# Turning the query tiles by VectorE's 32x32 squares and by their writes, in a hybrid attention layer

## The chip, the cores and the metric

One core of a Trainium2 chip runs the whole layer. The metric is the device time of one execution in microseconds (us).

## The reference

One layer of a diffusion backbone, in float32. A prompt tile of 128 tokens and 1024 latent tokens (eight tiles of 128) go through a modulated RMS norm and one input projection, whose columns belong to two mixers with 8 query heads, 2 key heads and head size 64 each. Mixer A attends over all latent and cached keys, mixer B within a window of 128 and the cached keys. The query part is this:

```python
p = h @ w_in
q_a, k_a, v_a, g_a, q_b, k_b, v_b, g_b = jnp.split(p, SPLIT_IDX, axis=-1)
q_a = rmsnorm(q_a.reshape(b, t, N_HEADS_A, HEAD_DIM), qn_a)      # the same for q_b
q_a = apply_rope(q_a, cos, sin)                                  # latent tokens alone
s = jnp.einsum('bqkgd,bskd->bkgqs', qblk, k_all) * (d ** -0.5)   # 4 query heads for each key head
p = jax.nn.softmax(s, axis=-1)
o = jnp.einsum('bkgqs,bskd->bqkgd', p, v_all)
```

The gated outputs of both mixers go through one output projection and are added to the stream.

## The kernel before

**Precision.** Float32 operands are split into a high part, rounded for TensorE's fast float32 format (`F32R`), and a low part, the rest. A product is made of three matmuls: high by high, high by low, low by high.

**Stages.** Modulation and the turned inputs (`hT`); the gates of mixer A; the query stage, 18 blocks (9 tiles for mixer A, then 9 for B, each time the tiles 1 to 8 and the prompt, tile 0, last); 9 key and value blocks; the gates of mixer B; then the attention in 36 units (tile, mixer, key head), with the output projection woven in.

**Order.** Nothing is reordered: at the end `in_order` ties every engine's instructions, the DMA issues of SyncE's queue among them, to the order in which the program wrote them. That order comes from an agenda. `block` counts two ticks, at the head and in the middle of its 24 matmuls (8 slices of the inner dimension by three), and `later(n, f)` runs `f` at the n-th tick from now. So a step of tile k is written between the matmuls of a later block. What a block of another weight needs (`split`: a high part by ScalarE, a low part by VectorE, 8 of each) is written into the last block of the weight before.

**A query tile** (`query`). The projection of 128 tokens by 8 heads by 64 lies in PSUM (`pq`). Its steps follow at the ticks of `QUERY_AT`, counted from one tick after the block:

- `squares` (0): ScalarE squares, VectorE sums them per head (`ss`, L717) and scales (`ms`, L184), GpSimd takes the power -1/2 (`rs_q`, L186).
- `scale` (2): VectorE multiplies by it (`qn`, L722) and makes the products with the rotation's tables (`ra` L657, `rb` L663).
- `rotated` (3): VectorE adds them into `qf` (L733), heads in pairs.
- `turned` (6): TensorE turns `qf` in four transposes of 128x128 into the bank `ptq` (L743), ScalarE copies the high part out (`qo0`, L746), two DMAs from ScalarE's queue write it to `q_dram`; one tick later VectorE subtracts the low part (`qo1`, L751), and after two more ScalarE's queue writes it in two DMAs.

The last tile of mixer B uses `QUERY_LAST` in place of `QUERY_AT`. So at any time three or four tiles are under way, and in a block VectorE works on one tile's `qn`, `ra`, `rb`, the next one's sum and an older one's `qf` and low part. `pq` rotates over six banks, `qf` over three buffers, `qo0` and `qo1` over two each.

`q_dram[t][m]` has 128 rows: 64 high and 64 low ones, one per element of a head; its columns are two groups of 512, one for each key head. A group is four heads of 128 tokens, head by head.

**Loads within the stage.** All are issued by SyncE's queue. At the head of the last but one block of mixer A (block 7) the program writes: two loads of the gate weights `wg` (1 MB each, L703), their bias (L777), the eight slices `rawqb` of mixer B's query weights (256 KB each, L234) and mixer B's rotation tables `tcos` and `tsin` (L671); two ticks later VectorE multiplies the tables by the gains (L672). The same place in mixer B has the 16 loads of `rawkv`. In blocks 12 and 16 stand the gate rows (`pgate` on TensorE, L696, and a sum of four steps on VectorE, L689).

**A unit** loads its group of `q_dram` (`u_load`, L977) into `qtile`, 128 rows by 512. For mixer A the running maxima (`pmx`, L997) take a head's 128 columns as the stationary operand; the scores (`st`, L1333 and L1334) stream all 512 columns against the keys, and their exponentials, times the values, give `pv`, 512 columns in the same order. `gated` (L1382) reads `pv` and the inverse sums `rs` by head pair into the output layout. For mixer B the scores (`sn`, L1085 and L1086) take a head's columns as the stationary operand.

Of the kernel before, what the change touches and what calls it, by code (L numbers as in the profile page):

```python
# [9 lines left out]
F32 = mybir.dt.float32  # L10
# [8 lines left out]
P = 128  # L19
D = 1024  # L20
KT = D // P
HD = 64
# [34 lines left out]
TURN = (2, 1)  # L57
PUT_LOW = 2
QUERY_AT = (0, 2, 3, 6)
PAD = 2  # L60
SECOND_FROM = 5
WARM = (12, 2, 1, 3)
# [14 lines left out]
PROMPT_KEYS_AT = 12  # L77
KV_ORDER = [0] + list(range(1, NT))
GATE_AT = (3, 7)
QUERY_LAST = (0, 1, 2, 5)  # L80
CACHE_AT = 8
VC_AT = 6
ONES_AT = 14
# [34 lines left out]
def hybrid_step(ctx, tc, x_prompt, x_sample, cache_k_a, cache_v_a, cache_k_b, cache_v_b,  # L118
# [100 lines left out]
    class Weights:  # L219
# [36 lines left out]
        def split(self):  # L256
            self.split_high()
            self.split_low()
# [418 lines left out]
    with tc.tile_pool(name="qt", bufs=2, side="right") as qt:  # L677
# [29 lines left out]
        def query(pq, m, t, tabs, n=1):  # L707

            nm = f"q{m}_{t}"
            pqv = pq.rearrange("p (h d) -> p h d", d=HD)  # L710
            v = {}

            def squares():
                sq = qt.tile([P, 8, HD], F32, tag="sq", name=f"sq{nm}")
                nc.scalar.activation(sq, pqv, AF.Square)
                ss = qt.tile([P, 8], F32, tag="ss", name=f"ss{nm}")
                nc.vector.tensor_reduce(ss, sq, axis=AX.X, op=ALU.add)  # L717
                v["r"] = rsqrt_mean(qt, ss, HD, 8, nm)

            def scale():  # L720
                qn = qt.tile([P, 8, HD], F32, tag="qn", name=f"qn{nm}")
                nc.vector.tensor_tensor(qn, pqv, v["r"].unsqueeze(2).to_broadcast([P, 8, HD]), op=ALU.mult)  # L722
                v["qn"] = qn
                if t:
                    v["rot"] = rope_products(qt, qn, 8, *tabs[m], t, nm)

            def rotated():

                qf = qt.tile([P, 4, 2, HD], F32, tag="qf", name=f"qf{nm}", bufs=3)
                out = qf.rearrange("p h g d -> p g h d")  # L730
                pair = lambda a: a.rearrange("p (g h) d -> p g h d", g=2)
                if t:
                    nc.vector.tensor_tensor(out, *(pair(a) for a in v["rot"]), op=ALU.add)  # L733
                else:
                    nc.vector.tensor_tensor(
                        out, pair(v["qn"]), gain4[:, 2 * m, :].unsqueeze(1).unsqueeze(1).to_broadcast([P, 2, 4, HD]),
                        op=ALU.mult)
                v["qf"] = qf

            def turned():  # L740
                ptq = bank_tr(f"pt{nm}")
                for h in range(4):
                    nc.tensor.transpose(ptq[:, P * h : P * h + P], v["qf"][:, h].rearrange("p g d -> p (g d)"),  # L743
                                        ident_r.bitcast(F32))
                qo = [qt.tile([P, 512], F32R, tag=f"qo{i}", name=f"qo{i}{nm}") for i in range(2)]
                nc.scalar.copy(qo[0], ptq)  # L746
                put(qo[0], 0)
                later(1, lambda: low(ptq, qo))

            def low(ptq, qo):  # L750
                nc.vector.tensor_tensor(qo[1], ptq, qo[0], op=ALU.subtract)  # L751
                later(PUT_LOW, lambda: put(qo[1], 1))

            def put(part, i):
                for g in range(2):
                    nc.scalar.dma_start(q_dram[t][m][64 * i : 64 * i + 64, 512 * g : 512 * g + 512],
                                       part[64 * g : 64 * g + 64].bitcast(F32))

            for d, f in zip(QUERY_LAST if (m, t) == (1, 0) else QUERY_AT, (squares, scale, rotated, turned)):
                later(n + d, f)  # L760

        tabs = {0: rope_tables(qt, 0, 2)}
# [210 lines left out]
    def u_load(i):  # L973
# [3 lines left out]
        nc.sync.dma_start(qt_.bitcast(F32), q_dram[t][m][:, 512 * g : 512 * g + 512])  # L977
        qtile[i] = qt_

    def max_items(i):  # L980

        t, m, g = units[i]
        out = []

        def item(h, b):
            if h == 0 and b == 0:
                mxtile[i] = qs.tile([P, 4, 3], F32, tag="mx", name=f"mx{i}", bufs=3)
            mx = mxtile[i]
            lhs = qtile[i][:, P * h : P * h + P]
            pm = bank("B" if i == APART + 1 else "A", f"pmx{i}_{h}_{b}")  # L990
            if t == 0:
                for h in range(4):
                    hs = slice(P * h, P * h + P)
                    nc.tensor.matmul(pm[:, hs], qtile[i][:, hs], khb[:, g, 0, :], start=True, stop=True)
                nc.vector.tensor_reduce(mx[:, :, 0], pm.rearrange("p (h n) -> p h n", h=4), axis=AX.X, op=ALU.max)
            else:
                nc.tensor.matmul(pm[:, 0:384], lhs, kha[:, g, 3 * b : 3 * b + 3, :], start=True, stop=True)  # L997
                nc.vector.tensor_reduce(mx[:, h, b : b + 1], pm[:, 0:384], axis=AX.X, op=ALU.max)  # L998

        def finish():  # L1000
            qb_ = qp.tile([68, 512], F32R, tag="qb", name=f"qb{i}", bufs=2)
            nc.sync.dma_start(qb_[0:64, :].bitcast(F32), q_dram[t][m][0:64, 512 * g : 512 * g + 512])
            qbtile[i] = qb_
            mx = mxtile.pop(i)
            mn = m_nat[i // 2 % 2]
            nc.vector.tensor_reduce(mn, mx if t else mx[:, :, 0:1], axis=AX.X, op=ALU.max)
            later(TURN[boxed(t)], transpose)

        def transpose():
            pt = bank("E" if i in EARLY else "A", f"ptm{i}")  # L1010
            nc.tensor.transpose(pt[0:4, 0:P].bitcast(F32R), m_nat[i // 2 % 2], ident_r)
            nc.vector.tensor_tensor(qbtile[i][64:68, :].rearrange("p (h n) -> p h n", h=4),
                                    pt[0:4, 0:P].unsqueeze(1).to_broadcast([4, 4, P]),
                                    diag.unsqueeze(2).to_broadcast([4, 4, P]), op=ALU.mult)

        for h in range(4 if t else 1):
            for b in range(3 if t > 0 else 1):
                out.append(lambda h=h, b=b: item(h, b))
        return out, finish

    def boxed(t):

        return t > 1
# [5 lines left out]
    def weight_items(i):  # L1029
# [48 lines left out]
        def item(h, early):  # L1078
            p0, p1_ = window(t)
            n = P * (p1_ - p0)  # L1080
            if i not in penat:
                first(n)
            lhs = qtile[i][:, P * h : P * h + P]
            s = bank("DEEE"[h] if i == 3 else "B" if early else "A", f"sn{i}_{h}")[:, 0:n]
            nc.tensor.matmul(s, lhs, khb[:, g, p0:p1_, :], start=True, stop=False)  # L1085
            nc.tensor.matmul(s, lhs, klb[:, g, p0:p1_, :], start=False, stop=True)  # L1086
            m0 = P if t == 1 else 0

            nc.vector.tensor_tensor_reduce(s, s, mask[:, m0 : m0 + n], -1.0, nsink[:, 4 * g + h : 4 * g + h + 1],  # L1089
                                           op0=ALU.add, op1=ALU.min, accum_out=v["nm"][:, h : h + 1])  # L1090
            later(1, lambda: exp(h, s, -1.0))

        def prompt():
            first(P)
            s = bank("A", f"sn{i}")
            for h in range(4):
                hs = slice(P * h, P * h + P)
                nc.tensor.matmul(s[:, hs], qtile[i][:, hs], khb[:, g, 1, :], start=True, stop=False)
                nc.tensor.matmul(s[:, hs], qtile[i][:, hs], klb[:, g, 1, :], start=False, stop=True)
            mx = small("mx4")  # L1100
            nc.vector.tensor_reduce(mx, s.rearrange("p (h n) -> p h n", h=4), axis=AX.X, op=ALU.max)
            nc.vector.scalar_tensor_tensor(v["nm"], mx, -1.0, nsink[:, 4 * g : 4 * g + 4], op0=ALU.mult, op1=ALU.min)
            for h in range(4):
                exp(h, s[:, P * h : P * h + P], 1.0)
# [242 lines left out]
    def values(i, b, last, blk, ph, pl):  # L1347
# [26 lines left out]
        def gated():  # L1374
            rs = v["rs"]
            o = 768 + 256 * (i % 3)
            of = spare[:, o : o + 256].rearrange("p (c n) -> p c n", c=2)
            a = 4 if m and boxed(t) else 1
            pvv, srv = (x.rearrange("p (c a s n) -> p s c a n", c=2, a=a, s=2) for x in (pv[0:64, :], rs))
            ofv = of.rearrange("p c (a n) -> p c a n", a=a)  # L1380
            for s in range(2):
                nc.vector.tensor_tensor(ofv[64 * s : 64 * s + 64], pvv[:, s], srv[:, s],  # L1382
                                        op=ALU.add if m else ALU.mult)
            nc.gpsimd.tensor_tensor(of, of, sgl.pop(i), op=ALU.mult)
            later(GATE_LATE, lambda: load_gate(i + 2 + (i + 2 >= APART)))
            if i + 3 == APART:
                later(GATE_LATE, lambda: load_gate(APART))
            v["of"] = of
# [208 lines left out]
```

## Time and profile before

| | |
|---|---|
| median of 3 runs | 685.09 us (681.66, 685.09, 685.44) |
| the profiled execution | 684.31 us, its span 682.5 us, granted clock 0.999 |
| busy: TensorE, VectorE, ScalarE, GpSimd | 671.6, 492.9, 403.9, 374.3 us |
| query stage's transposes L743 | 72, first at 103.0, last at 205.8 us |
| VectorE in 100 to 155 and 155 to 208 us | 42.43 of 55, 42.16 of 53 us busy |
| DMA engines in these two stretches | 0.38 and 0.60 busy |

In the profile's rows PE is TensorE's matmuls, PEld its stationary loads, DVE is VectorE, ACT ScalarE, POOL GpSimd, SP SyncE; a `q` behind the name is the engine's own queue, where DMAs are issued. A row of a group has its line, engine, operation, output and inputs, shapes and count, then busy us and mean ns, then the idle time before and what ended it. A row of a timeline or of the chain begins with its start in us from the span's start and its length. A row of the waits has who waited for whom: us in total, times, the longest. A row of the windows has the stretch, its length, busy us and instructions of PE, PEld, DVE, ACT and POOL, the granted clock, the share of the DMA engines and GB/s.

### The profile page before, as it was taken

How to read it: one execution, taken by the hardware profiler on the slowest of the kernel's cores; microseconds unless marked ns; L12 is line 12 of the kernel's file. 1: busy time of each engine (PE TensorE's matmuls, PEld its weight loads, DVE VectorE, ACT ScalarE, POOL GpSimd, SP SyncE). 2: the span in 40 equal slices, each digit the busy share in tenths (PEclk: the TensorE clock that was granted, in tenths of full speed). 3: DMA queues.
4: the chain of work that ended last, by engine and by line, in shares of the span. 5: the costliest groups of instructions: out<-in, count | busy, mean ns of one | idle time of the engine just before them, and what ended most of it. 6: DMA issues, size and time to landing. Idle time of an engine off the chain costs nothing.

```text
span 682.5 us, 10639 instructions
## 1 busy us (share of the span) xinstructions
PE 671.6 (98%) x3325; PEld 535.8 (79%) x3325; DVE 492.9 (72%) x1060; ACT 403.9 (59%) x834; POOL 374.3 (55%) x379
## 2 busy tenths in 40 slices
PE   8999999999999999999999999999999999999987
PEld 4678988878788888997767777877777777777766
DVE  4777247877787882856788788788787877886673
ACT  6656412411233243169778877987798778878760
POOL 2557023332222240248687669767876778778761
PEclk9999999999999999999999999999999999999999
DMA  9961283339445024542266445764565545644623
GB/s 351 405 250 76 79 313 75 78 84 301 120 119 142 29 90 144 183 136 64 81 195 187 154 149 169 195 191 129 162 192 156 154 148 171 201 123 147 185 61 125
DMA packets 75851, 107.74 MB, mean 158 GB/s; under 512 B 9296, under 2 KB 43532, under 8 KB 75796
## 3 DMA queue, kind: packets, MB, share of 16 engines
q1 hardware_dynamic: 67556, 95.11, 43.6%
q10 hardware_dynamic: 8240, 11.96, 6.5%
q8 instruction: 26, 0.43, 0.3%
q14 instruction: 29, 0.24, 0.1%
HBM read 73.24 MB, written 33.80 MB: 157 GB/s over the span
## 4 chain that ended last, share of the span: by engine, by line
PE 92%; DVE 3%; ACT 2%; DMA 1%; issue 1%; POOL 0%; SPq 0%; ACTq 0%; DVEq 0%
PE po L1434 14%; PE pv L1357 7%; PE pv L1354 6%; PE pmx L997 5%; PE pq L270 5%; PE pq L268 5%; PE pq L269 5%; PE pv L1356 5%; PE st L1333 5%; PE st L1334 5%; PE pg L282 3%; PE pg L278 3%; PE pg L283 3%; PE pk L269 2%; PE pk L270 2%; PE pk L268 2%
## 5 line engine op out<-in xcount | busy, mean ns | idle before, releaser
L1344 POOL TENSOR_TENSOR pl<-pe,ph 128x512 fp32r<-128x512 f32 x129 | 167.0, 1301 | 71.8 <-ACT ph L1340 46.0
L998 DVE TENSOR_REDUCE mx<-pmx 128x1 f32<-128x384 f32 x192 | 100.0, 547 | 28.9 <-PE pmx L997 28.8
L1336 ACT ACTIVATE pe<-st 128x512 f32<-128x512 f32 x146 | 86.6, 593 | 12.8 <-PE st L1334 12.0
L1340 ACT CAST ph<-pe 128x512 fp32r<-128x512 f32 x146 | 90.7, 621 | 5.6
L1354 PE MATMUL pv<-ph,v_hi 128*128 128x512 f32 x208 | 82.1, 395 | 0.6 <-DVE spare L1382 0.5
L1357 PE MATMUL pv<-pl,v_hi 128*128 128x512 f32 x208 | 82.2, 395 | 0.2 <-DVE pl L1330 0.2
L186 POOL TENSOR_TENSOR rs_q<-ms_q,mhalf 128x8 f32<-128x8 f32 x18 | 34.2, 1899 | 80.7 <-DVE ms_q L184 80.7
L1434 PE MATMUL po<-wo,ogh 128*128 128x512 f32 (+1 forms) x224 | 73.2, 387 | 0.0
L1055 ACT ACTIVATE pen<-sn,nm 128x512 f32<-128x512 f32 (+2 forms) x72 | 45.0, 626 | 37.3 <-DVE nm L1089 33.5
L1089 DVE CUSTOM_DVE_ANT_0 sn<-sn,mask,nsink 128x512 f32<-128x512 f32 (+1 forms) x64 | 45.9, 717 | 19.3 <-PE sn L1086 12.8
L997 PE MATMUL pmx<-kha,qt 128*128 128x384 f32 x192 | 58.5, 351 | 0.6 <-DVE mx L998 0.6
L1356 PE MATMUL pv<-ph,v_lo 128*64 128x512 f32 x146 | 57.7, 395 | 0.0
L1333 PE MATMUL st<-qt,kha 128*128 128x512 f32 x144 | 57.7, 400 | 0.0
L1334 PE MATMUL st<-qb,kla 68*128 68x512 f32 x144 | 57.4, 398 | 0.0
L1357 PEld LDWEIGHTS pv<-pl,v_hi 128*128 128x128 f32 x208 | 39.1, 188 | 17.5 <-DVE pl L1330 0.6
L997 PEld LDWEIGHTS pmx<-kha,qt 128*128 128x128 f32 x192 | 36.3, 189 | 14.0 <-ACT pen L1055 3.6
L1354 PEld LDWEIGHTS pv<-ph,v_hi 128*128 128x128 f32 x208 | 39.1, 188 | 8.9 <-PE pmx L997 0.9
L1434 PEld LDWEIGHTS po<-wo,ogh 128*128 128x128 f32 x224 | 41.0, 188 | 5.7 <-ACT ogh L1396 0.3
L746 ACT CAST qo0q<-ptq 128x512 fp32r<-128x512 f32 x18 | 10.6, 586 | 57.5 <-PE ptq L743 51.6
L1434 PE MATMUL po<-wo,ogl 128*128 128x512 f32 (+1 forms) x112 | 43.5, 388 | 0.0
L1322 POOL TENSOR_TENSOR pl<-pen,ph 128x512 fp32r<-128x512 f32 x28 | 37.4, 1337 | 7.4 <-ACT ph L1318 7.4
L1065 DVE STREAM_TRANSPOSE pen<-pen 128x512 f32<-128x512 f32 (+1 forms) x56 | 37.0, 677 | 5.8 <-ACT pen L1055 5.7
(258 smaller groups left out, 1721.9 us busy)
## 6 DMA issues: line engine op xcount, KB each, us to landing
td<-pen SPq DMA_DIRECT2D x24, 512.0 KB
pen<-td SPq DMA_DIRECT2D x96, 128.0 KB
qt<-qd SPq DMA_DIRECT2D x36, 256.0 KB
wm<-in_w_mod_ss_dram SPq DMA_DIRECT2D x7, 1024.0 KB
qd<-qo0q ACTq DMA_DIRECT2D x36, 128.0 KB
qd<-qo1q ACTq DMA_DIRECT2D x36, 128.0 KB
sgl<-gd SPq DMA_DIRECT2D x35, 128.0 KB
out_dram<-yt SPq DMA_DIRECT2D x17, 256.0 KB
```

Of the source, the lines that this page charges most:

```text
L268: nc.tensor.matmul(out, h_at(0, i, k, tok), w.hi[k], start=(k == 0), stop=False)
L997: nc.tensor.matmul(pm[:, 0:384], lhs, kha[:, g, 3 * b : 3 * b + 3, :], start=True, stop=True)
L998: nc.vector.tensor_reduce(mx[:, h, b : b + 1], pm[:, 0:384], axis=AX.X, op=ALU.max)
L1333: nc.tensor.matmul(s, kh, qtile[i], start=True, stop=False)
L1334: nc.tensor.matmul(s, kl, qbtile[i], start=False, stop=True)
L1336: nc.scalar.activation(pe, s, AF.Exp)
L1340: nc.scalar.copy(ph, pe)
L1344: nc.gpsimd.tensor_tensor(pl, pe, ph, op=ALU.subtract)
L1354: nc.tensor.matmul(pv, two, ph, start=(b == 0), stop=False)
L1356: nc.tensor.matmul(pv[0:64, :], vl, ph, start=False, stop=False)
L1357: nc.tensor.matmul(pv, two, pl, start=False, stop=last)
L1434: nc.tensor.matmul(po[n, q.start], a, wo_parts[KT * n + k][lo][:, q], start=(k == KS[0] and p == 0), stop=(k == KS[-1] and p == 2))
```

## The change

For the 18 query tiles the transposes on TensorE go. `rotated` now writes `qf` in two adds, one for each key head, with the four heads of a group innermost (a step of four elements between neighbours of one head). `boxes_turned` turns 32x32 squares of it in place on VectorE, taking every fourth element. `split` makes the high part on ScalarE and the low part on GpSimd, both from SBUF. `put_boxes` puts the squares where they belong: four DMAs for each part, one for each 32 tokens, in pieces of 512 bytes, the high part's from ScalarE's queue and the low part's from SyncE's. The steps stand at ticks 0, 2, 3, 4 and 5 (`BOXED_AT`), for the last tile at 0 to 4, and the low put two ticks after the split.

In `q_dram` a group's 512 columns are now tokens with the four heads innermost. `head(i, h)` therefore reads every fourth column of `qtile` as a stationary operand; the maxima's rows in `qbtile` and, for mixer A, the reads of `pv` and `rs` in `gated` follow that order.

```diff
-QUERY_LAST = (0, 1, 2, 5)
+BOXED_AT = (0, 2, 3, 4, 5)
+MIXED = (0, 1)
+QUERY_LAST = (0, 1, 2, 3, 4)
...
             def rotated():
-                qf = qt.tile([P, 4, 2, HD], F32, tag="qf", name=f"qf{nm}", bufs=3)
-                out = qf.rearrange("p h g d -> p g h d")
-                pair = lambda a: a.rearrange("p (g h) d -> p g h d", g=2)
+                qf = qt.tile([P, 512], F32, tag="qf", name=f"qf{nm}", bufs=3)
+                v["qf"] = qf
+                pair = lambda a: a.rearrange("p (g h) (b j) -> p g h b j", g=2, b=2)
+                if m in MIXED:
+                    out = qf.rearrange("p (g b j h) -> p g h b j", g=2, b=2, h=4)
...
+                for g in range(2):
+                    if t:
+                        nc.vector.tensor_tensor(out[:, g], *(pair(a)[:, g] for a in v["rot"]), op=ALU.add)
...
+            def boxes_turned():
+                at = v["qf"].rearrange("p (b x h) -> p b h x", b=4, h=4)
+                nc.vector.transpose(at, at)
+
+            def split():
+                qo = [qt.tile([P, 512], F32R, tag=f"qo{i}", name=f"qo{i}{nm}") for i in range(2)]
+                nc.scalar.copy(qo[0], v["qf"])
+                put_boxes(qo[0], 0, nc.scalar)
+                nc.gpsimd.tensor_tensor(qo[1], v["qf"], qo[0], op=ALU.subtract)
+                later(PUT_LOW, lambda: put_boxes(qo[1], 1, nc.sync))
+
+            def put_boxes(part, i, queue):
+                out = q_dram[t][m][64 * i : 64 * i + 64].rearrange("(b j) (g a x) -> a j g b x", b=2, g=2, a=4)
+                for a in range(4):
+                    src = part[32 * a : 32 * a + 32].bitcast(F32).rearrange("p (g b x) -> p g b x", g=2, b=2)
+                    queue.dma_start(out[a], src)
...
+            if m in MIXED:
+                at, last = QUERY_LAST if (m, t) == (1, 0) else BOXED_AT, (boxes_turned, split)
+            else:
+                at, last = QUERY_AT, (turned,)
+            for d, f in zip(at, (squares, scale, rotated) + last):
                 later(n + d, f)
...
+    def head(i, h):
+        if units[i][1] in MIXED:
+            return qtile[i].rearrange("p (n h) -> p h n", h=4)[:, h]
+        return qtile[i][:, P * h : P * h + P]
...
-            lhs = qtile[i][:, P * h : P * h + P]
+            lhs = head(i, h)
...
-            nc.vector.tensor_tensor(qbtile[i][64:68, :].rearrange("p (h n) -> p h n", h=4),
-                                    pt[0:4, 0:P].unsqueeze(1).to_broadcast([4, 4, P]),
-                                    diag.unsqueeze(2).to_broadcast([4, 4, P]), op=ALU.mult)
+            nc.vector.tensor_tensor(qbtile[i][64:68, :].rearrange("p (n h) -> p n h", h=4),
+                                    pt[0:4, 0:P].unsqueeze(2).to_broadcast([4, P, 4]),
+                                    diag.unsqueeze(1).to_broadcast([4, P, 4]), op=ALU.mult)
...
+            if m == 0:
+                pvv, srv = (x.rearrange("p (n c s) -> p s c n", c=2, s=2) for x in (pv[0:64, :], rs))
+                ofv = of
```

More of the change, by code (lines that the diff above doesn't have):

```diff
@@ L727, in rotated @@
             def rotated():
-                qf = qt.tile([P, 4, 2, HD], F32, tag="qf", name=f"qf{nm}", bufs=3)
-                out = qf.rearrange("p h g d -> p g h d")
-                pair = lambda a: a.rearrange("p (g h) d -> p g h d", g=2)
-                if t:
-                    nc.vector.tensor_tensor(out, *(pair(a) for a in v["rot"]), op=ALU.add)
-                else:
-                    nc.vector.tensor_tensor(
-                        out, pair(v["qn"]), gain4[:, 2 * m, :].unsqueeze(1).unsqueeze(1).to_broadcast([P, 2, 4, HD]),
-                        op=ALU.mult)
@@ L738, in rotated @@
-                v["qf"] = qf
+                qf = qt.tile([P, 512], F32, tag="qf", name=f"qf{nm}", bufs=3)
[3 more added lines that the diff above has]
+                    out = qf.rearrange("p (g b j h) -> p g h b j", g=2, b=2, h=4)
+                else:
+                    out = qf.rearrange("p (h g b j) -> p g h b j", g=2, b=2, h=4)
+                for g in range(2):
+                    if t:
+                        nc.vector.tensor_tensor(out[:, g], *(pair(a)[:, g] for a in v["rot"]), op=ALU.add)
+                    else:
+                        gain = gain4[:, 2 * m, :].rearrange("p (b j) -> p b j", b=2).unsqueeze(1)
+                        nc.vector.tensor_tensor(out[:, g], pair(v["qn"])[:, g], gain.to_broadcast([P, 4, 2, 32]),
+                                                op=ALU.mult)
@@ L742, in turned @@
                 for h in range(4):
-                    nc.tensor.transpose(ptq[:, P * h : P * h + P], v["qf"][:, h].rearrange("p g d -> p (g d)"),
+                    nc.tensor.transpose(ptq[:, P * h : P * h + P], v["qf"][:, P * h : P * h + P],
                                         ident_r.bitcast(F32))
@@ L757, in put @@
                                        part[64 * g : 64 * g + 64].bitcast(F32))
-            for d, f in zip(QUERY_LAST if (m, t) == (1, 0) else QUERY_AT, (squares, scale, rotated, turned)):
+            if m in MIXED:
+                at, last = QUERY_LAST if (m, t) == (1, 0) else BOXED_AT, (boxes_turned, split)
+            else:
+                at, last = QUERY_AT, (turned,)
+            for d, f in zip(at, (squares, scale, rotated) + last):
                 later(n + d, f)
@@ L993, in item @@
                     hs = slice(P * h, P * h + P)
-                    nc.tensor.matmul(pm[:, hs], qtile[i][:, hs], khb[:, g, 0, :], start=True, stop=True)
+                    nc.tensor.matmul(pm[:, hs], head(i, h), khb[:, g, 0, :], start=True, stop=True)
                 nc.vector.tensor_reduce(mx[:, :, 0], pm.rearrange("p (h n) -> p h n", h=4), axis=AX.X, op=ALU.max)
@@ L1082, in item @@
                 first(n)
-            lhs = qtile[i][:, P * h : P * h + P]
+            lhs = head(i, h)
             s = bank("DEEE"[h] if i == 3 else "B" if early else "A", f"sn{i}_{h}")[:, 0:n]
@@ L1097, in prompt @@
                 hs = slice(P * h, P * h + P)
-                nc.tensor.matmul(s[:, hs], qtile[i][:, hs], khb[:, g, 1, :], start=True, stop=False)
-                nc.tensor.matmul(s[:, hs], qtile[i][:, hs], klb[:, g, 1, :], start=False, stop=True)
+                nc.tensor.matmul(s[:, hs], head(i, h), khb[:, g, 1, :], start=True, stop=False)
+                nc.tensor.matmul(s[:, hs], head(i, h), klb[:, g, 1, :], start=False, stop=True)
             mx = small("mx4")
@@ L1377, in gated @@
             of = spare[:, o : o + 256].rearrange("p (c n) -> p c n", c=2)
-            a = 4 if m and boxed(t) else 1
-            pvv, srv = (x.rearrange("p (c a s n) -> p s c a n", c=2, a=a, s=2) for x in (pv[0:64, :], rs))
-            ofv = of.rearrange("p c (a n) -> p c a n", a=a)
+            if m == 0:
+                pvv, srv = (x.rearrange("p (n c s) -> p s c n", c=2, s=2) for x in (pv[0:64, :], rs))
+                ofv = of
+            else:
+                a = 4 if boxed(t) else 1
+                pvv, srv = (x.rearrange("p (c a s n) -> p s c a n", c=2, a=a, s=2) for x in (pv[0:64, :], rs))
+                ofv = of.rearrange("p c (a n) -> p c a n", a=a)
             for s in range(2):
```

## The prediction

> **What bounds the kernel now.** I read the page's shares of busy time, then the chain of work that ended last, then TensorE's waits, then the timelines of the query stage (81 to 207 us) engine by engine, SyncE's queue included.
>
> ```profile
> PE 671.6 (98%) x3325; PEld 535.8 (79%) x3325; DVE 492.9 (72%) x1060; ACT 403.9 (59%) x834; POOL 374.3 (55%) x379
> PE 92%; DVE 3%; ACT 2%; DMA 1%; issue 1%; POOL 0%; SPq 0%; ACTq 0%; DVEq 0%
> ...
> 132.83 0.44 PE ptq L743 x4
> 138.76 0.44 PE ptq L743 x4
> 152.48 0.59 PE ptq L743 x4
> 190.21 0.44 PE ptq L743 x4
> PEld pk L269 <- DVE wlokv L252: 0.5, 1, 0.5
> ```
>
> TensorE is the bound and hardly waits, so what leaves its queue is time won unless another engine or a load is then late. The last line is the one place of the query stage where something already is late: VectorE's low halves of the key and value weights (wlokv), by 0.5 us. Next, what VectorE does in one block of the stage:
>
> ```profile
> 115.31 0.69 DVE L722 TENSOR_TENSOR qnq<-pq,rs_q 128x512 f32<-128x512 f32 x1 [0.93 <-POOL rs_q L186]
> 116.04 0.69 DVE L657 TENSOR_TENSOR ra_q<-qnq,tcos 128x512 f32<-128x512 f32 x1
> 116.65 0.75 DVE L663 TENSOR_TENSOR rb_q<-qnq,tsin 128x256 f32<-128x256 f32 x2
> 117.90 0.69 DVE L717 TENSOR_REDUCE ssq<-sqq 128x8 f32<-128x512 f32 x1 [0.50 <-ACT sqq L715]
> 118.62 0.17 DVE L184 TENSOR_SCALAR ms_q<-ssq 128x8 f32<-128x8 f32 x1
> 118.70 0.68 DVE L733 TENSOR_TENSOR qfq<-ra_q,rb_q 128x512 f32<-128x512 f32 x1
> 119.30 0.68 DVE L751 TENSOR_TENSOR qo1q<-ptq,qo0q 128x512 fp32r<-128x512 f32 x1
> 120.91 0.69 DVE L722 TENSOR_TENSOR qnq<-pq,rs_q 128x512 f32<-128x512 f32 x1 [0.93 <-POOL rs_q L186]
> ...
> 125.23 0.69 DVE L672 TENSOR_TENSOR tcos<-tcos,gain 128x512 f32<-128x512 f32 x1
> 125.85 0.68 DVE L672 TENSOR_TENSOR tsin<-tsin,gsw 128x512 f32<-128x512 f32 x1
> ...
> 130.57 1.29 DVE L252 TENSOR_TENSOR wloqb<-rawqb,whiqb 128x512 fp32r<-128x512 f32 x2
> 182.15 2.85 DVE L689 TENSOR_TENSOR bg<-pgate,bg 2x512 f32<-2x512 f32 x4
> ```
>
> From start to start: qn 0.73, ra 0.61, rb 0.67 (1.25 here, less the 0.50 wait and some latency), sum of squares 0.72, ms 0.08, so 2.8 us; then GpSimd's power is awaited, and the next qn starts 2.29 after ms. A round is 5.1. A block takes TensorE 5.93 with its transposes (132.83 is followed by 138.76) and 5.49 without. In each round VectorE has 0.93 idle, in the wait for the power.
>
> I number the stage's blocks 0 to 17, tile k being that of block k. Mixer B starts with block 9; the key blocks follow block 17. Tile k's transposes stand now at the head of block k+4, so those at 132.83 are tile 5's, at the head of block 9, and those at 190.21 are tile 14's, at the head of the first key block.
>
> **The change, part by part.**
>
> *Transposes gone.* The chain gives each tile's four 0.44 us, and twice 0.59 (behind the gate rows): 16 x 0.44 + 2 x 0.59 = 8.2 us, all on the path.
>
> *VectorE, per tile.* A subtract goes, 0.60 from start to start. A transpose of 128x512 comes, and the add becomes two of 256 (L663's pair: 0.67, against 0.61 for one of 512).
>
> ```profile
> L1065 DVE STREAM_TRANSPOSE pen<-pen 128x512 f32<-128x512 f32 x48 | 32.5, 695 | 4.6 <-ACT pen L1055 4.5
> L998 DVE TENSOR_REDUCE mx<-pmx 128x1 f32<-128x384 f32 x192 | 100.0, 547 | 28.9 <-PE pmx L997 28.8
> L1344 POOL TENSOR_TENSOR pl<-pe,ph 128x512 fp32r<-128x512 f32 x129 | 167.0, 1301 | 71.8 <-ACT ph L1340 46.0 <-PE st L1334 25.3 <-DMA td<-pen 0.4
> L1320 DVE TENSOR_TENSOR pl<-pen,ph 128x512 fp32r<-128x512 f32 x26 | 29.8, 1147 | 3.9 <-ACT ph L1318 3.9
> L1342 DVE TENSOR_TENSOR pl<-pe,ph 128x512 fp32r<-128x512 f32 x17 | 12.1, 712 | 22.3 <-POOL ex L1107 19.9 <-ACT ph L1340 2.5
> ```
>
> No row of this kernel touches every fourth element (16 bytes apart), as the new transpose and the add's writes do. Lower end: L1065's 0.70. Upper end: twice the price of an element, which is about 1.1 ns (690 ns for L717's 512, 547 for L998's 384), so 0.55 more: 1.25, and the add 0.55 more too. I take 0.70, the row of the same operation. Add and transpose then make 1.4 us, less than the 2.29 of the power: they cost nothing while that covers them, and their full length where it doesn't, behind weight splits and gate sums.
>
> *GpSimd.* A subtract, 1.30, between the powers. It stands behind the power of the tile two later and so delays none, but it runs beside VectorE's ra. Two such subtracts side by side cost VectorE between nothing and 1147 - 712 = 435 ns; I take 0.2 a round: 5.3 against a block's 5.49. VectorE keeps pace, but a lag shrinks by 0.2 a round, where now it is 0.8.
>
> *ScalarE.* The copy reads SBUF in place of PSUM; four high puts replace two high and two low ones. Nothing, beside TensorE. The puts write the same bytes in pieces of 512 bytes in place of 2 KB; nothing in this stage waits for them. If they were slow, the next subtract would wait for its buffer.
>
> *SyncE's queue.* The low puts move here, four per tile, and this term decides. Now nothing on this queue waits during mixer A, and it runs far ahead of the blocks:
>
> ```profile
> 85.72 1.90 SPq L703 DMA_DIRECT2D wg<-in_w_mod_g_dram  x2
> 90.40 7.54 SPq L234 DMA_DIRECT2D rawqb<-in_w_in_dram  x8
> 97.99 0.43 SPq L671 DMA_DIRECT2D tcos<-in_k_cos_dram  x1
> 160.98 9.68 SPq L234 DMA_DIRECT2D rawkv<-in_w_in_dram  x16
> ...
> 98.00:102.00 4.00, 4.00 (x19) 3.30 (x19) 2.43 (x6) 0.39 (x1) 2.02 (x1) 1.00 0.96 368
> 102.00:106.00 4.00, 4.00 (x21) 3.30 (x20) 2.42 (x6) 1.10 (x2) 1.95 (x1) 1.00 0.18 49
> ```
>
> The first three lines stand in the program at the head of block 7, behind the low puts of tiles 0 to 2. Tile 2's put waits for its subtract, and that stands on GpSimd behind the power of tile 4, which ends at 115.3 (the qn at 115.31 is tile 4's). With 0.4 of contention before it the subtract ends at 117.0; four issues at 0.43 to 118.7. From the first issue (85.72) to the end of the batch's traffic (368 GB/s before 102, 49 after) are 16.3 us, so mixer B's tables (tcos, tsin) land near 135; with 4.6 MB at 368 GB/s and no other delay it is 12.5 us and 131. I take 134.5, near the row as it ran.
>
> Queued on VectorE is L672, which multiplies the tables; it stands at the middle of block 7 and would be reached at 125, as now. VectorE works in order, so it stands still till 134.5. Then L672 1.2, the transpose of tile 5 0.7, tile 6 from qn to ms 2.8: the first wloqb starts at 139.2 and ends at 139.85. TensorE wants it in block 9, which starts at 133.27 now and, without six sets of transposes, at 130.6: for its second matmul, at 130.85. It waits 9.0 us. From there to the first key block are now 190.65 - 133.27 = 57.4, without nine sets (7 x 0.44, 2 x 0.59) 53.1: 139.6 + 53.1 = 192.7, where it is 190.65.
>
> Does VectorE keep up till then? From the first wloqb at 139.2: eight splits at 0.6, add and transpose 0.7 each, 6.2, so tile 7's qn at 145.4. To tile 15's: five rounds of 5.3, one of 3.6 (the prompt's, without rotation), two with a gate sum (2.8 + 2.85 + 1.4 + 0.2 = 7.25, the power is hidden), 44.6. Then 3.0 to wlokv: 193.0, done 193.7, wanted at 192.9. That is 0.8, 0.3 more than today; without contention nothing, with 435 ns a round 2.6.
>
> rawkv will stand behind the low put of tile 11, near 180, and its ten us of issues end at 190; the last of it is wanted near 198. Nothing, with some us to spare.
>
> *Heads innermost in the units.* 344 stationary loads read columns 16 bytes apart, and L1382 reads PSUM and SBUF so for mixer A.
>
> ```profile
> L997 PEld LDWEIGHTS pmx<-kha,qt 128*128 128x128 f32 x192 | 36.3, 189 | 14.0 <-ACT pen L1055 3.6 <-DVE mx L998 3.5 <-DVE qb L1012 0.2
> L1356 PEld LDWEIGHTS pv<-ph,v_lo 128*64 128x64 f32 x146 | 19.6, 134 | 4.4
> L1382 DVE TENSOR_TENSOR spare<-pv,rs 64x256 f32<-64x256 f32 x64 | 26.4, 413 | 0.5
> ```
>
> ```profile
> 423.90 0.34 PE L997 MATMUL pmx<-kha,qt 128*128 128x384 f32 x1
> 424.08 0.63 PE L1434 MATMUL po<-wo,ogh 128*128 128x512 f32 x2
> 424.54 0.39 PE L1354 MATMUL pv<-ph,v_hi 128*128 128x512 f32 x1
> ```
>
> 64 columns less make a load 55 ns shorter, so 128 are about 0.11 us; doubled, 0.22. Under a matmul of 512 columns (424.08 to 424.54 are two, 0.23 each) that stays hidden, under one of 384 (0.18) 0.04 shows. Four of a unit's twelve follow another, 64 in all, and the prompt's 24 follow matmuls of 128: 64 x 0.04 + 24 x 0.11 = 5 us doubled, nothing as it is. I take nothing, the row of the same load. L1382: nothing, or 32 x 0.28 us on VectorE beside TensorE's work.
>
> **Sum.** 684.31 (the profiled execution, 0.8 under the median shown, 685.09) - 8.2 + 9.0 + 0.3 = 685.4; on the median's footing **686.2**.
>
> **Rivals.**
> *The loads are in time*, and it ends on the other side: the 9.0 goes, 8.2 stays: 676.9, up to 2.5 more with contention. For it: the product, transpose and round behind L672 are short, 4.7; against: the order of SyncE's queue is the program's. It decides at a landing before 130.2 - 4.7 = 125.5; between that and 134.5 each us is one us.
>
> *Every fourth element costs double.* Add and transpose make 2.5, a little over the power: 0.2 more in five rounds, 1.1 in two gate rounds, 1.6 at block 9, 0.3 for the prompt's, so 5.1; the last tiles, loads and L1382 some 4 more: 685.4 + 9.1, 695.3 on the median's footing. For it: no row shows such a step at the plain price; against it none either. [...]
>
> *Stationary loads at four times*, 0.44: 0.2 shown at each of some 320, 64 us: 750. No row speaks for it.
>
> **How the numbers follow.** Chances: forecast 0.42, loads in time 0.22, double 0.32, fourfold 0.04. The forecast's own range is 682 (landing at 131) to 690 (full contention, a later landing). The range of 677 to 699 leaves out the fourfold case and the outer ends of the second and third. Within 0.5%, about what can't be told from no change here, is 681.7 to 688.5. Faster: nearly all of the second case and a little of the first, 0.23; same: most of the first, 0.33; slower: the rest, 0.44.
>
> **What would show it.** Right: wg and rawqb issued after 117 on SyncE's queue; VectorE idle before L672 until a DMA; TensorE waiting for wloqb; no ptq in the chain. Wrong: mixer B's first block without a wait (then the loads were in time), a transpose of 1.2 us or stationary loads over 0.2 (then the step costs), TensorE waiting in the attention for mx or spare.

## The result and the profile after

The changed kernel takes 707.19 us (706.72 to 707.51, four runs) where the kernel before takes 685.27 beside it: a ratio of 1.0337, 95% interval 1.031 to 1.0365. It is 22 us slower; 686.2 was forecast, with a range of 677 to 699.

Profile after, the page's head and engines:

```profile
span 705.6 us, 10674 instructions
...
PE 681.2 (97%) x3253; PEld 557.8 (79%) x3253; DVE 517.4 (73%) x1078; ACT 405.3 (57%) x834; POOL 394.1 (56%) x397
```

TensorE has 72 matmuls fewer and is busy 9.6 us longer, its stationary loads 22 us longer. Where the time went is read from the stretches of mixer A's projection, mixer B's, the keys, the gates of B and the attention. First the kernel before:

```profile
81.00:133.00 52.00, 52.00 (x243) 43.01 (x242) 35.17 (x74) 12.83 (x24) 15.65 (x9) 1.00 0.48 153
133.00:190.00 57.00, 57.00 (x283) 44.40 (x282) 43.85 (x84) 13.31 (x24) 15.56 (x9) 1.00 0.58 164
190.00:244.00 54.00, 53.98 (x256) 44.19 (x255) 43.60 (x127) 18.39 (x46) 17.11 (x17) 1.00 0.32 87
244.00:296.00 52.00, 52.00 (x306) 47.68 (x305) 32.15 (x74) 12.67 (x39) 11.57 (x9) 1.00 0.44 143
296.00:682.00 386.00, 378.91 (x1723) 296.51 (x1721) 291.55 (x610) 299.16 (x610) 279.13 (x282) 1.00 0.50 152
```

Then the changed kernel:

```profile
80.00:129.00 49.00, 49.00 (x218) 40.63 (x217) 34.71 (x68) 10.57 (x19) 18.80 (x13) 1.00 0.38 119
129.00:196.00 67.00, 55.75 (x251) 42.65 (x250) 59.63 (x102) 16.09 (x28) 27.60 (x18) 0.90 0.56 162
196.00:255.00 59.00, 55.49 (x241) 44.49 (x240) 46.04 (x131) 18.73 (x46) 22.54 (x21) 0.94 0.33 90
255.00:309.00 54.00, 54.00 (x305) 49.70 (x304) 32.31 (x74) 12.66 (x39) 11.49 (x9) 1.00 0.43 138
309.00:705.00 396.00, 389.33 (x1723) 320.34 (x1722) 297.61 (x610) 299.78 (x610) 278.45 (x282) 1.00 0.49 148
```

There are two losses. Mixer B and the keys lose 10 and 5 us: TensorE stands 11.25 of 67 and 3.5 of 59 us, at a granted clock of 0.90 and 0.94. The gates of B and the attention lose 2 and 10 us without TensorE being less busy: the same number of matmuls takes longer. Mixer A alone gains, 3 us.

**The queue.** SyncE's queue in the changed kernel:

```profile
104.13 12.99 SPq L761 DMA_DIRECT2D qd<-qo1q  x12
117.16 1.19 SPq L705 DMA_DIRECT2D wg<-in_w_mod_g_dram  x2
...
122.74 6.97 SPq L236 DMA_DIRECT2D rawqb<-in_w_in_dram  x8
129.76 0.43 SPq L673 DMA_DIRECT2D tcos<-in_k_cos_dram  x1
```

The loads stand behind the twelve low puts of tiles 0 to 2, and VectorE and TensorE wait for them (VectorE's timeline, then TensorE's waits):

```profile
134.93 0.69 DVE L674 TENSOR_TENSOR tcos<-tcos,gain 128x512 f32<-128x512 f32 x1 [12.33 <-DMA tcos<-in_k_cos_dram]
...
136.45 1.09 DVE L748 STREAM_TRANSPOSE qfq<-qfq 128x512 f32<-128x512 f32 x1
...
140.19 1.30 DVE L254 TENSOR_TENSOR wloqb<-rawqb,whiqb 128x512 fp32r<-128x512 f32 x2
```

```profile
PE pq L271 <- DVE wloqb L254: 11.3, 1, 11.3
PE pk L271 <- DVE wlokv L254: 1.4, 2, 0.8
...
PE pk L270 <- ACT whikv L247: 1.1, 1, 1.1
...
PE ptk L911 <- DVE k2k L857: 1.0, 1, 1.0
```

And the idle time costs more than itself. The windows around it, with the granted clock as the last column but two:

```profile
137.00:140.00 3.00, 0.00 (x0) 0.00 (x0) 2.96 (x6) 0.62 (x1) 0.00 (x0) 0.50 0.25 66
140.00:143.00 3.00, 2.06 (x5) 1.68 (x6) 2.97 (x8) 1.86 (x4) 2.57 (x2) 0.50 0.26 68
143.00:146.00 3.00, 3.00 (x10) 2.18 (x9) 3.00 (x5) 1.85 (x4) 1.19 (x1) 0.61 0.08 22
146.00:149.00 3.00, 3.00 (x14) 2.46 (x14) 2.96 (x5) 0.62 (x1) 0.00 (x0) 1.00 0.26 66
```

The clock is still 0.50 when TensorE starts again; until 145.4 its matmuls begin 0.43 us apart in place of 0.23, some 2 us for ten of them.

**The step of 16 bytes.** The groups of the changed kernel:

```profile
L748 DVE STREAM_TRANSPOSE qfq<-qfq 128x512 f32<-128x512 f32 x18 | 20.3, 1126 | 0.4
L740 DVE TENSOR_TENSOR qfq<-ra_q,rb_q 128x256 f32<-128x256 f32 x32 | 17.5, 632 | 0.0
L659 DVE TENSOR_TENSOR ra_q<-qnq,tcos 128x512 f32<-128x512 f32 x16 | 13.5, 842 | 0.5
L1030 PEld LDWEIGHTS pmx<-kha,qt 128*128 128x128 f32 x192 | 55.9, 310 | 9.5 <-DVE mx L1031 3.9 <-ACT pen L1088 0.2
L1118 PEld LDWEIGHTS sn<-khb,qt 128*128 128x128 f32 x64 | 19.9, 310 | 4.7 <-ACT pen L1088 0.6 <-issue 0.2
L1419 DVE TENSOR_TENSOR spare<-pv,rs 64x256 f32<-64x256 f32 x64 | 32.6, 510 | 0.5
```

The transpose takes 1126 ns where 695 was taken, a stationary load 310 where it took 189, the output's `gated` (now L1419) 510 where it took 413. VectorE's `ra` goes from 692 to 842 beside GpSimd's new subtract. What the load does to TensorE is seen where two matmuls of 384 columns and an output matmul follow each other; before, and after:

```profile
326.64 0.51 PE L997 MATMUL pmx<-kha,qt 128*128 128x384 f32 x2
326.99 0.39 PE L1434 MATMUL po<-wo,ogl 128*128 128x512 f32 x1
```

```profile
340.13 0.57 PE L1030 MATMUL pmx<-kha,qt 128*128 128x384 f32 x2
340.54 0.40 PE L1471 MATMUL po<-wo,ogl 128*128 128x512 f32 x1
```

From the first start to the output matmul the pair takes 0.41 in place of 0.35. Over the attention, from the start times in the two traces: a `pmx` followed by an output matmul takes 225 ns on average, not 187 (78 times), by a value matmul 295, not 214 (36 times), a `sn` followed by another 264, not 214 (78 times). These three make 9.7 of the ten us. In the gates of B a `pmx` followed by a gate matmul takes 268 ns, not 175 (23 times): 2.1 us, the loss of that stage. Behind most matmuls of 512 columns the load is hidden, and they stay 0.23 apart; of the 48 `sn` pairs of 512 columns 35 do, and the other 13 go from 0.29 to 0.34 us to 0.41 to 0.46.

### The profile page after: what moved, and what is told of

It is laid out like the page before. It is cut to its first block, busy times and chain, and to the rows that moved or that the text cites. A ratio compares the mean times of both kernels' runs of the same rounds, so it can differ in the third digit from the quotient of the medians.

```text
span 705.6 us, 10674 instructions
## 1 busy us (share of the span) xinstructions
PE 681.2 (97%) x3253; PEld 557.8 (79%) x3253; DVE 517.4 (73%) x1078; ACT 405.3 (57%) x834; POOL 394.1 (56%) x397
## 5 line engine op out<-in xcount | busy, mean ns | idle before, releaser
L188 POOL TENSOR_TENSOR rs_q<-ms_q,mhalf 128x8 f32<-128x8 f32 x18 | 31.6, 1756 | 73.7 <-DVE ms_q L186 59.3
L1030 PE MATMUL pmx<-kha,qt 128*128 128x384 f32 x192 | 66.6, 392 | 1.2 <-DVE mx L1031 1.2
L1030 PEld LDWEIGHTS pmx<-kha,qt 128*128 128x128 f32 x192 | 55.9, 310 | 9.5 <-DVE mx L1031 3.9
L717 ACT ACTIVATE sqq<-pq 128x512 f32<-128x512 f32 x18 | 10.8, 598 | 60.9 <-PE pq L272 32.5
L271 PE MATMUL pq<-wloqb,h 128*128 128x512 f32 x72 | 29.2, 405 | 11.3 <-DVE wloqb L254 11.3
```

## The experiments

The theories: (1) the order of SyncE's queue, (2) the 16-byte step of the units' stationary loads, with the same step on VectorE beside it. Rivals are named with each run. Ratios are against the kernel before on the same chip, with 95% intervals.

**Loads early**, all else as changed:

```diff
-if (m, t) in ((0, ts[-2]), (1, ts[GATE_AT[0]])):      # wg, bg
+if (m, t) in ((0, ts[0]), (1, ts[GATE_AT[0]])):
-if t == ts[-2]:                                       # rawqb, tables
+if t == ts[0 if m == 0 else -2]:
-    tabs[1] = rope_tables(qt, 2, 2)
+    tabs[1] = rope_tables(qt, 2, 16)
```

> The changed kernel, but the gate's weights, mixer B's weights and the tables of mixer B are issued at the head of block 0, ahead of all low puts on SyncE's queue (the products with the gain stay where they are). The key and value weights stay behind the low puts. Theory 1 (queue order): the 11.25 us wait for wloqb and the half clock after it go; mixer B's nine blocks take 53 in place of 66.8, so 707.2 - 13.7 = 693.5, between 690 and 697, and the attention stays 396. Rival (VectorE's longer rounds, from the 16-byte step and the work beside GpSimd, make wloqb late anyway): TensorE still waits over 5 us in mixer B, and the time stays over 700.

Measured: 696.87 us, 1.019 (1.0167 to 1.0213), 1.5% or 10 us less than the changed kernel. A window of mixer B, then TensorE's waits:

```profile
129.00:185.00 56.00, 54.00 (x250) 40.99 (x249) 54.68 (x95) 15.23 (x26) 27.05 (x18) 1.00 0.54 155
```

```profile
PE ptk L911 <- DVE k2k L857: 3.5, 1, 3.5
PE pk L271 <- DVE wlokv L254: 1.9, 3, 0.8
PE pq L271 <- DVE wloqb L254: 1.7, 2, 1.1
```

The long wait and its half clock are gone (granted clock 1.00 in this window): theory 1 holds. Mixer B takes 56, not 53: VectorE is busy 54.68 of the 56 us and has no time left, so small waits remain.

The keys gain nothing: 185 to 245 is 60 us. ScalarE in this stage:

```profile
187.10 3.22 ACT L247 CAST whikv<-rawkv 128x512 fp32r<-128x512 f32 x6 [3.49 <-DMA qd<-qo0q]
206.72 0.38 ACT L836 ACTIVATE sqk<-pk 128x256 f32<-128x256 f32 x1 [2.61 <-DMA qd<-qo0q]
```

The high halves of the key and value weights (`whikv`), and the squares of the second key block (`sqk`), stand behind ScalarE's own issues of the four high puts of a tile, 2.5 us or more each time. VectorE waits 3.7 us for these squares, and its copy of the prompt's keys (`k2k`), for which TensorE waits, comes behind their sum.

**Units strided, all else as before the change**: TensorE still transposes, and the copy and the subtract behind it write the columns with the heads innermost.

```diff
-nc.scalar.copy(qo[0], ptq)
+nc.scalar.copy(qo[0].rearrange("p (x h) -> p h x", h=4), ptq.rearrange("p (h x) -> p h x", h=4))
...
+def head(i, h):
+    return qtile[i].rearrange("p (n h) -> p h n", h=4)[:, h]
```

> The kernel before, with TensorE's transposes and the old puts, but with heads innermost in a unit's columns: ScalarE's copy and VectorE's subtract write the columns in that order, and the stationary loads, the maxima's row and mixer A's output rows read them so. Nothing else of the change is in it. Theory 2 (the 16-byte step of the stationary loads): the attention takes 395 to 397 in place of 386, TensorE goes from start to start in 0.23 instead of 0.18 behind each 384-column matmul with such a load, and the time is 685.3 + 9.5 = 695, with up to 2 more from the strided writes of the query stage. Rival (the attention's ten us come from something else of the change: units that arrive later, another order of work, VectorE): the time is within 2 us of the kernel before, and the steps stay 0.18.

Measured: 696.47 us, 1.0179 (1.0158 to 1.0201), as theory 2 expects.

```profile
L1000 PEld LDWEIGHTS pmx<-kha,qt 128*128 128x128 f32 x192 | 55.9, 310 | 9.5 <-DVE mx L1001 4.6 <-ACT pen L1058 0.5
```

The load takes 310 ns here too, and the attention 396 us as in the changed kernel. The units' columns alone cost 1.8%, 12 us. With the queue's 10 this is the whole of the 22 us; so, by this subtraction, the 8.2 us of the transposes were spent elsewhere in the query and key stages.

**Smaller steps.** The next five kernels have the loads early and the heads in pairs (8 bytes from column to column) or one after another (4 bytes). The puts then have pieces of 256 or 128 bytes, and the 64 rows of a part were interleaved in DRAM to keep them at four. At first a unit came back in two DMAs.

```diff
-at = v["qf"].rearrange("p (b x h) -> p b h x", b=4, h=4)
+at = v["qf"].rearrange("p (c x) -> p c x", c=16)            # 4 bytes; 8: "p (c x w) -> p c w x", w=2
...
+for k in range(2):
+    nc.sync.dma_start(qt_[64 * k : 64 * k + 64].bitcast(F32),
+                      q_dram[t][m][64 * k : 64 * k + 64, 512 * g : 512 * g + 512].rearrange("(j b) n -> b j n", b=2))
```

> As the first kernel of this call (loads early), and the heads stand in pairs: columns 8 bytes apart in the square transposes, in the adds and in the stationary loads; the pieces of the puts are 256 bytes; a row of 64 in DRAM is stored with its halves interleaved, so that the puts stay four, and a unit is loaded by two DMAs. [...] If the price goes with the distance: transpose about 0.85, stationary load 0.23 to 0.25, the attention 389 to 392, 681 to 686. If any step costs what 16 bytes cost: 690 to 694.

> As the first kernel of this call (loads early), with head after head in a unit's columns: every element of the transpose, the add (one of 512 again) and the stationary loads is next to the last; the pieces of the puts are 128 bytes, four times as many as in the changed kernel; units are loaded by two DMAs as in the kernel with pairs. Theories 1 and 2 together: transpose 0.70, add 0.68, stationary load 0.19, attention 386; 685.3 - 8.2 = 677 and up to 3 more for the late key and value weights: 676 to 680. Rival (the small pieces of the puts or GpSimd's subtract beside VectorE cost as much as the step): over 684.

Measured: 792.49 us, 1.1585 (1.1549 to 1.1621), and 797.40, 1.1658 (1.1626 to 1.169). Neither theory had this. TensorE's waits with 4 bytes, and a window while the two loads of a unit and little else run:

```profile
PE sn L1114 <- DMA qt<-qd: 46.7, 12, 5.7
```

```profile
338.50:340.00 1.50, 1.50 (x8) 1.27 (x7) 1.40 (x4) 1.47 (x5) 0.56 (x2) 1.00 0.13 46
```

The units come late; 0.13 of the 16 DMA engines, about two, is busy. My first reading was that the second load is held until the first has landed. One load then replaced the two, with halves and parts interleaved in the rows:

```diff
+rows = q_dram[t][m].rearrange("(j k b) n -> k b j n", k=2, b=2)
+nc.sync.dma_start(qt_.bitcast(F32), rows[:, :, :, 512 * g : 512 * g + 512])
```

> As the kernel with head after head in a unit's columns and the loads early (797 us), but a row of 64 lies in DRAM so (halves and parts innermost in the rows) that a unit is loaded by one DMA again, in place of two into one tile. Theory 3 (the second of two loads into the same tile was held until the first had landed, and with it everything behind it on SyncE's queue): the waits for qt and pen go, the attention is 386 and the time 676 to 680, as it was expected of that kernel. Rival (pieces of 128 bytes, or the order of the rows, make the loads slow): still over 740.

> The same mending for the heads in pairs, 8 bytes from column to column (792 us with two loads). [...] If the price grows with the distance: the transpose near 0.85, the load 0.23 to 0.25, and 3 to 8 us more than with 4 bytes.

> The kernel with 4 bytes and one load, and the key and value weights also ahead: they are issued at the fourth block of mixer B in place of the eighth. If what is left of the queue's order still costs at the key blocks (wlokv late, and the half clock after a wait of some us), it is 1 to 4 us faster than the kernel with 4 bytes and one load, near 676; if VectorE alone makes wlokv late, within 1 us of it. Both against the kernel before: 1.0 to 1.4% faster.

Measured: 714.12 us, 1.0448 (1.0407 to 1.049); 709.90, 1.0381 (1.0345 to 1.0417); 718.41, 1.0514 (1.049 to 1.0538). All three miss. A window of the first during a unit load:

```profile
395.00:396.00 1.00, 1.00 (x6) 0.82 (x5) 1.00 (x2) 0.97 (x3) 1.00 (x2) 1.00 0.27 98
```

Now 0.27 of the engines, about four, is at work. The load's two outer dimensions, k and b, have two entries each and together step through four neighbouring rows; in the kernels of the last paragraph the outermost had two. So in these two windows about as many engines work as the load has outer entries (0.13 of 16 is 2.1, 0.27 is 4.3), if k and b count as one dimension of four. That a second load was held can't be the whole reason: the maxima's operand `qb` is one load, still with two outer entries, and TensorE's longest wait in the first kernel is now for it:

```profile
PE st L1362 <- DMA qb<-qd: 12.4, 11, 2.9
```

The third kernel shows the other side of the queue. With the key and value weights ahead of the puts the puts are late, GpSimd's subtract waits for its buffer (1.4 us in the first kernel, 5.8 here), and wlokv is not earlier but later (0.7 there, 5.7 here); the waits of GpSimd in this stage, and of TensorE:

```profile
POOL qo1q L749 <- DMA qd<-qo1q: 5.8, 1, 5.8
```

```profile
PE pk L271 <- DVE wlokv L254: 5.7, 1, 5.7
```

**Whole rows.** A unit is again one DMA of 128 consecutive rows; the elements of a head stay interleaved, and the keys are put in the same order.

```diff
+nc.sync.dma_start(qt_.bitcast(F32), q_dram[t][m][:, 512 * g : 512 * g + 512])
...
-nc.vector.tensor_tensor(k2, *(two(a) for a in v["rot"]), op=ALU.add)
+for a in range(2):
+    out = k2[:, :, a].rearrange("p i (j b) -> p i b j", b=2)
+    nc.vector.tensor_tensor(out, *(halves(x) for x in v["rot"]), op=ALU.add)
```

> Head after head in a unit's columns (4-byte step), the loads early, and now a unit is one DMA of 128 whole consecutive rows, as in the kernel before: the order of the 64 elements of a head is interleaved in DRAM, and the keys' elements are put in the same order by VectorE's last key step (8-byte step, two instructions in place of one). Theory 3, as it stands after the last runs (a DMA whose outermost dimension has 2 or 4 entries is worked on by about 2 or 4 of the 16 DMA engines, so units came late): unit loads land within 3.7 us, the waits for qt and qb go, gates B take 52, the attention 386; mixer B and the keys stay as in the last kernels (55.7 and 56): 678.8 + 1.8 = 680.6, between 678 and 684, 0.1 to 0.9% faster than before. Rival (the pieces of 128 bytes or the order of the rows slow the loads): waits for qt stay, over 700.

> The same with the heads in pairs (8-byte step in transposes, adds and stationary loads). The transpose showed 0.71 at 8 bytes as at 4, the load 0.20 against 0.19. Within 2 us of the kernel with 4 bytes if 8 bytes cost nothing; 690 and more if the loads' 10 ns show behind every matmul.

Measured: 683.41 us, 1.0005 (0.9983 to 1.0026), and 682.15, 0.9981 (0.9961 to 1.0002). Groups of the first and of the second, and a window of the second during a unit load:

```profile
L1027 PEld LDWEIGHTS pmx<-kha,qt 128*128 128x128 f32 x192 | 36.3, 189 | 15.0 <-DVE mx L1028 4.6 <-ACT pen L1085 3.3 <-DVE qb L1042 0.2
...
L743 DVE STREAM_TRANSPOSE qfq<-qfq 128x512 f32<-128x512 f32 x18 | 12.8, 709 | 0.5
```

```profile
L1029 PEld LDWEIGHTS pmx<-kha,qt 128*128 128x128 f32 x192 | 37.6, 196 | 14.2 <-DVE mx L1030 4.1 <-ACT pen L1088 3.2 <-DVE qb L1044 0.2
...
L745 DVE STREAM_TRANSPOSE qfq<-qfq 128x512 f32<-128x512 f32 x18 | 12.8, 712 | 0.5
```

```profile
384.40:385.40 1.00, 1.00 (x6) 0.83 (x5) 0.97 (x3) 0.97 (x3) 1.00 (x1) 1.00 0.84 236
```

The attention is back at 386 us, as both texts expect, and the puts still have pieces of 128 and 256 bytes, so these were not what made the loads slow: in the window 0.84 of the DMA engines is busy. A step of 8 bytes costs nothing measurable in the time (682.15 us against 683.41 with 4); one of 16 bytes costs some 60% on VectorE's transpose (1126 ns against 709 and 712) and on the stationary load (310 against 189 and 196). Against the kernel with the loads early the step is worth some 2%; 1.8% of it is the units' (above), so on VectorE it was nearly hidden, as far as subtracting runs tells.

**What eats the 8.2 us.** In the 8-byte kernel the gates and the attention are as before the change. By TensorE's start times the projections of both mixers take 103.7 us in place of 109.2, where 15 of the 18 sets of transposes (6.9 us) stood, but the keys take 59.0 in place of 54.3. TensorE's longest wait there, behind which the granted clock is 0.50 from 206.6 to 210.0 (its mean from 200 to 216 is 0.89):

```profile
PE ptk L911 <- DVE k2k L856: 3.0, 1, 3.0
```

Two kernels from the 4-byte one with whole rows ("the first kernel" of their texts): the high puts on SyncE's queue too (`put_boxes(qo[0], 0, nc.sync)`, the key weights two blocks earlier, `ts[-4]` for `ts[-2]`; the text says three), and the low part by VectorE (`nc.vector.tensor_tensor(qo[1], v["qf"], qo[0], op=ALU.subtract)` one tick later).

> As the first kernel of this call, but the high puts are issued on SyncE's queue too, not ScalarE's, and the key and value weights three blocks earlier to make up for it. If ScalarE's issues (2.0 us a tile) are what makes the squares of the first key block and so the prompt's keys late, the wait for k2k (2.4 us and its half clock) goes: 676 to 679. If the queue is a zero-sum game (what is moved ahead holds up the puts, then GpSimd's subtract for want of a buffer, then the powers): slower than the first kernel by 2 us or more.

> As the first kernel of this call, but the low part is subtracted by VectorE one step later, as before the change, not by GpSimd. If GpSimd's subtract beside VectorE costs 0.35 in ra and delays the power behind it, VectorE's ra is back at 0.69 and a round is no longer than 5.3 us in spite of the 0.6 more: within 1.5 us of the first kernel, either side. If VectorE is short of time in mixer B: 2 to 6 us slower.

Measured: 695.27 us, 1.0173 (1.0126 to 1.022): the queue is a zero-sum game. From 125 to 205 us GpSimd waits 20.2 us for the buffer of its subtract and VectorE 14.5 us for the powers; then TensorE waits 8.0 us for wlokv. And 686.85, 1.0051 (1.0037 to 1.0064), 3.4 us more than with GpSimd; its `ra`, against 896 ns with GpSimd beside it:

```profile
L659 DVE TENSOR_TENSOR ra_q<-qnq,tcos 128x512 f32<-128x512 f32 x16 | 11.1, 692 | 0.5
```

So GpSimd's subtract does cost VectorE 0.2 us a round on average, and is still the cheaper place: without transposes on TensorE a block lasts 5.4 us (nine in the 49 of mixer A), and VectorE is short of time.

**Towards a better kernel**, from the 8-byte one:

```diff
+if (m, t) == (0, ts[0]):                   # tables first
+    tabs[1] = rope_tables(qt, 2, 5)
...
-put_boxes(qo[0], 0, nc.scalar)
+put_boxes(qo[0], 0, nc.sync if m and t in ts[-3:] else nc.scalar)     # last puts
...
-kn = kt.tile([P, 4, HD], F32, tag="kn", name=f"kn{nm}", bufs=1)
+kn = kt.tile([P, 4, HD], F32, tag="kn", name=f"kn{nm}", bufs=2)       # last kernel alone
```

> From the kernel with 8-byte steps and whole rows (682.2): mixer B's tables are loaded ahead of the gate's and mixer B's weights, and multiplied with the gain in block 2 in place of block 7. If the 1.3 us of these products right ahead of mixer B are what makes wloqb late there (2 us with the slower start of TensorE's next matmuls), mixer B begins without a wait: 680 to 681.5. If VectorE's lag has built up over the rounds before: no change, 682.

> From the kernel with 8-byte steps and whole rows (682.2): the high puts of the last three query tiles are issued on SyncE's queue. If ScalarE's issues ahead of the prompt's key squares make k2k late (3.0 us at TensorE, with the transposes and the slower start behind it), the wait shrinks to under 1 us and the time to 679 to 680. If VectorE or GpSimd is late there in any case: within 0.7 us of 682.

> Both of the last two together: their gains add, 677 to 679.5, which is 0.6 to 1.0% faster than the kernel before; if the lags are one and the same lag of VectorE, the better of the two alone.

> From the kernel with both (680.3): in the two kernels with the last high puts on SyncE's queue VectorE stands 6.8 us at the key scaling, since the prompt's keys go out from the one scaled tile by a DMA that is issued behind these puts. Here there are two such tiles. If that is the wait, the 2.7 us for k2k at TensorE go: 677 to 678.5, 0.8 to 1.0% faster than the kernel before. If the next thing is late by as much: 679.5 to 680.5.

Measured: 681.12 us, 0.9961 (0.9944 to 0.9979); 681.11, 0.9959 (0.9943 to 0.9974); both 680.27, 0.9948 (0.9927 to 0.9969); with two tiles 680.75, 0.995 (0.9933 to 0.9968). The steps between these four are too small to be told apart; against the kernel before, both together are 0.5% faster, the best version found. The tables' time lies in the better case's range, but TensorE still waits 0.9 us for wloqb, as without that edit; the other three end above their better cases. Moving the puts cured one wait (VectorE's 4.0 us for the squares of the second key block in the 8-byte kernel) and made another, which the last edit moved on: TensorE's transposes of the keys still wait 1.5 and 1.7 us. VectorE with the last puts on SyncE's queue, then with two tiles:

```profile
206.98 0.86 DVE L843 SCALAR_TENSOR_TENSOR knk<-pk,rs_k,gain 128x64 f32<-128x64 f32 x4 [6.81 <-DMA out_dram<-knk]
```

```profile
205.36 0.86 DVE L843 SCALAR_TENSOR_TENSOR knk<-pk,rs_k,gain 128x64 f32<-128x64 f32 x4 [5.75 <-POOL rs_k L188]
```

## Why the prediction was wrong, point by point

- *Transposes gone, 8.2 us.* Right in size: mixer A takes 49 us, not 52; six of the 18 sets (2.6 us) stood there.
- *SyncE's queue, 9.0.* The mechanism was right, with the tables landing at 134.9 (134.5 was forecast) and wloqb starting at 140.2 (139.2). The wait was 11.25: TensorE came at 129.7, not 130.85, mostly since the stage began 0.9 us earlier, and the transpose ahead of wloqb took 1.1, not 0.7. The term left out the half clock after the wait, 2 us more. The loads-early run gives the queue's whole worth, 10 us.
- *rawkv, "nothing, with some us to spare"*, and *wlokv, 0.3.* Right. rawkv was issued from 183.8 to 194.5, later than forecast, behind low puts that mixer B's lateness had moved, but no split waits for it. VectorE's first low half came 0.8 us late, as worked out.
- *ScalarE, "nothing, beside TensorE".* This failed, at the keys. That stage lost 7.0 us against 52.5, its length of before without the last four tiles' transposes. From TensorE's start times: 3.5 us are the late weights (the 0.8 among them), 1.1 the prompt's keys, 2.4 matmuls at half clock (granted 0.50 from 200 to 206). The third high half of the weights starts at 198.9, when ScalarE has issued the four high puts of a tile (4.8 us idle); the squares of the second key block, and with them the prompt's keys, stand behind four more (2.9). The loads-early kernel shows the same two waits (3.5 and 2.6). What each is worth stays open: with the last high puts on SyncE's queue VectorE's wait for the squares was gone, and the next wait took its place.
- *Transpose 0.70 (bounds 0.70 to 1.25), add nothing (up to 0.55 more).* The upper bounds were near: 1.13, and the pair of adds takes 1.07, not 0.67. The choice by "the row of the same operation" failed: that row had the operation, not the step. As to the time it mattered little.
- *Stationary loads, nothing (doubled: 0.22, 5 us).* This is the step of the sum that failed most: it took "the row of the same load", which had no such step. A load takes 0.12 more, about the doubled case, and the gates and the attention 12 us more, against 5. The prompt's 24 matmuls came out as counted there (2.6 us; 2.5 measured). Mixer A's 64 at 0.04 (2.6 us) did not: the traces show about 0.05 at each of 114 `pmx` of the attention, and 0.09 at 23 in the gates of B, 8 us in all. The pairs of `sn` outside the prompt, another 2.2 us, were not counted.
- *L1382, up to 0.28 each.* 0.10, beside TensorE. *GpSimd's subtract, 0.2 a round*: 0.15 on average. Both right.
- *The rival "every fourth element costs double"*, 695.3, had the right cause. That such a step doubles the price, or makes a load four times as long, no run shows: the transpose took 1126 ns where smaller steps took 709 and 712, a load 310 where it had taken 189, 1.6 times each. It fell short by its loads, and by the half clock and the key stage, which no case had at this size; its 5.1 us on VectorE are more than the runs show, where the smaller steps save at most some 2 us beyond the units' 12.

The profiled execution's own sum closes: 684.3 - 8.2 - 0.9 (earlier start) + 11.25 + 2 (half clock) + 7.0 (keys) + 12.2 (gates and attention) = 707.7, against 707.4. The half clock was read from the traces and not tried by itself.

## What to carry to other kernels

A layout that helps one stage is paid by every later reader: count the readers' accesses, and price a 16-byte step by a measured row of that step, not of that operation. A stationary load is not always hidden: here one of 310 ns showed 0.04 to 0.09 us at matmuls of 384 columns and 0.12 at those of 128, so look for short matmuls next to it. Before a DMA is moved to a queue whose order the program fixes, list what stands behind it there, and behind the issues that stay on a compute engine; moving that ahead in turn delays the DMA (with the key and value weights ahead, GpSimd's subtract waited 5.8 us for a put, not 1.4). Here TensorE's waits of 3.0 and 11.25 us were followed by 3.4 and 4.4 us at a granted clock of 0.50.

## What the runs showed of the hardware

- A step of 16 bytes between float32 elements: square transpose of 128x512 1126 ns against 709 to 712 at 4 and 8 bytes; stationary load of 128x128 310 against 189 and 196.
- In one window each, unit loads with 2 outer entries kept 0.13 of the 16 DMA engines busy, one with two outer dimensions of 2 kept 0.27, one of 128 whole rows 0.84. The kernels with the first and the second took some 110 and 30 us more than with whole rows (in the second, the loads of `qb` still had 2).
- After 11.25 us without work TensorE ran at a granted clock of 0.50 for its first 4.4 us; after a wait of 3.0 us, in the 8-byte kernel, the clock was 0.50 for 3.4 us (0.89 on average from 200 to 216).
